# Half-height score passes made full-height, correction passes put in runs, and three order strings changed in a two-layer encoder

## The chip, the cores and the metric

The kernel runs on one core of a Trainium2 chip. Times are device microseconds (us) of that core, and lower is better. The core has a matrix engine (TensorE, PE in the rows; its weight loads stand apart as PEld), VectorE (DVE), ScalarE (ACT), GpSimd (POOL) and SyncE (SP, which issues the DMAs here).

## What is computed

A sequence of 256 tokens of width 1024 goes through two layers in fp32. Layer 0 mixes with a Hyena group (long convolutions by DFT) and eight heads of latent attention; layer 1 mixes with differential attention. Each layer then has a four-head cross-attention into 256 memory tokens and a squared-ReLU MLP of width 4096. What the change touches in layer 1:

```python
def diff_block_attention(q, k, v, lam):        # 16 half heads of width 64, 8 heads
    s = jnp.einsum('bqhd,bkhd->bhqk', qblk, k).astype(jnp.float32) * scale
    p = jax.nn.softmax(s, axis=-1).reshape(B, H, 2, Q_BLOCK, S)
    a = (p[:, :, 0] - lam * p[:, :, 1]).astype(v.dtype)      # two softmax maps a head
    return jnp.einsum('bhqk,bkhe->bqhe', a, v)
```

## The kernel before

**Arithmetic.** Nearly every product runs in a rounded fp32 format (fp32r) with a correction. An operand is split into `hi` (ACT rounds it, L110 or, with a gain, L105) and `lo` (DVE takes the rest, L111 or L106), and a product is hi·hi + hi·lo + lo·hi. `mm3` (L115 to L117) does this as three passes into one PSUM bank. A *pass* is one matmul instruction: a 128x128 weight tile is held and 128, 256 or 512 columns stream past.

**Side by side.** Where the moving operand is the activation (MLP up-projection, cross-attention queries, memory keys of layer 0), its `hi` and `lo` halves lie beside each other in 512 columns. `side_by_side` (L223 to L231) then needs two passes for a weight tile: one of 512 columns with the weight's `hi` (L229) and one of 256 columns with the weight's `lo` (L225). `proj_w4` calls it for four PSUM banks `c`, four weight groups `i` and two tiles `k` a group, bank by bank; `mem_k2` for two banks, two groups and four tiles. So a 512-column pass and a 256-column pass take turns. `joined` then adds the two halves of each bank on ACT and DVE. `Gained` splits the next stage's activation: three of its quarters as soon as they exist, the last one (`flush`) behind the first weight group of the next projection.

**Differential heads.** `qkv` turns q and k by position, transposes them (L886) and splits them into tiles `qkT`, in which one half head fills partitions 0 to 63 and its partner 64 to 127. `od_a` makes the two score maps of a head: for each token half `t` and each half head `m` one `mm3` on 64 partitions and 256 columns, twelve passes a head and 96 in all, into one bank for each `m`. A softmax (`softmax_e`) runs on each bank, and DVE combines the two maps with the factor lambda.

**Order.** Steps of a stage are named by letters, and strings set the order in which they are written (`ORDER_EVEN`, `ORDER_CROSS`, `ORDER_ODD`): in a cross-attention `Q` is a query projection, `K` and `V` keys and values of the memory, `S` the scores of a head, `B` its transposes (L455) and value product, `W` a part of the output projection; in the differential layer `Q` is `qkv`, `A`, `B`, `C` are the three steps of a head. A scheduler then lays the instructions on the engines' queues, and it moves filling work (memory keys of a later stage, weight splits) between them. The engines take their queues in order.

Of the kernel before, what the change touches and what calls it, by code (L numbers as in the profile page):

```python
# [10 lines left out]
F32 = mybir.dt.float32  # L11
BF16 = mybir.dt.bfloat16
F32R = mybir.dt.float32r
AF = mybir.ActivationFunctionType
ALU = mybir.AluOpType
AX = mybir.AxisListType

P = 128
D = 1024
EPS = 1e-6  # L20
SUBLN_EPS = 1e-5
# [3 lines left out]
C1 = 6.28125  # L25
C2 = float(np.float32(TWO_PI - C1))
C3 = float(np.float32(TWO_PI - C1 - C2))
PI_LO = 3.1415925

ORDER_EVEN = "X J H0 L U K G R S0 D H1 F0 S1 T0 S2 S3 P0 O0 O1 O2 H2 S4 O3 H3 T1 F1 S5 S6 O4 O5 Y S7 H4 P1 H5 O6 O7 M W"  # L30
ORDER_CROSS = [
    "Q0 V0 K0 K1 S0 B0 K2 S1 Q1 K3 S2 W0 V2 B1 S3 B2 B3 W1",
    "K0 K1 Q0 V0 S0 S1 K2 B0 Q1 K3 S2 V1 B1 V2 B2 W0 V3 S3 B3 W1",
]
ORDER_ODD = "Q2 Q0 Q1 A0 A1 B0 A2 C0 B1 B2 Q4 C1 C2 Q3 A3 A4 Q5 A5 B3 B4 C3 A6 C4 B5 B6 C5 A7 W0 W1 C6 B7 C7"


@with_exitstack
def tile_encoder(ctx: ExitStack, tc: tile.TileContext, a: dict, out: bass.AP):
    nc = tc.nc  # L40
# [19 lines left out]
    def wk():  # L60
        return T(ps, [P, 512], F32, "b", bufs=3)
# [47 lines left out]
    def split(hi, lo, src):  # L109
        nc.scalar.copy(hi, src)  # L110
        nc.vector.tensor_tensor(lo, src, hi.bitcast(F32), op=ALU.subtract)  # L111

    def mm3(o, l, r, first, last):
        (lh, ll), (rh, rl) = l, r
        nc.tensor.matmul(o, lh, rh, start=first, stop=False)  # L115
        nc.tensor.matmul(o, lh, rl, start=False, stop=False)  # L116
        return nc.tensor.matmul(o, ll, rh, start=False, stop=last)  # L117
# [28 lines left out]
    h = hilo()[:2]  # L146
    lat_all = t16(F32)
    lat_raw = [lat_all[:, i * 832:(i + 1) * 832] for i in range(4)]
    for c in range(2):
        for t in range(2):  # L150
            cs = slice(c * 512, (c + 1) * 512)
# [68 lines left out]
            if mid is not None and q == at:  # L220
                mid()

    def side_by_side(b, w, both, kk):  # L223
        def low():
            nc.tensor.matmul(b[:, :256], w[1], both[:, kk, 0, :], start=False, stop=False)  # L225

        if kk == 7:
            low()
        nc.tensor.matmul(v3(b, 2), w[0], both[:, kk], start=kk == 0, stop=kk == 7)  # L229
        if kk < 7:  # L230
            low()  # L231

    def proj_w4(h, src, banks, gi, mid=None):
        both = h[2]
        for i in range(4):
            wh, wl = (v3(z, 2) for z in weight(src[i], gi=(gi, 2 * i)))
            for c in range(4):
                for k in range(2):
                    side_by_side(banks[c], [z[:, k, c * P:(c + 1) * P] for z in (wh, wl)], both, 2 * i + k)
            if mid is not None and i == 0:  # L240
                mid()

# [41 lines left out]
    memB = T(cst, [P, 8, 2, 256], F32R, "memB")  # L284
# [9 lines left out]
    def mem_k2(l, u):  # L294
        bs = [wk(), wk()]
        for i in range(2):
            wh, wl = (v3(z, 4) for z in weight(a["xa_wk"][l, u, i]))
            for c in range(2):
                for k in range(4):
                    side_by_side(bs[c], [z[:, k, c * P:(c + 1) * P] for z in (wh, wl)], memB, 4 * i + k)  # L300
        y = joined(*bs)
        k = [T(rp, [P, 2, 256], F32R, f"kTm{i}", bufs=2) for i in range(2)]
        split(k[0], k[1], y)
        return k
# [122 lines left out]
        return (ec, es_), (pc, ps_)  # L427


    def softmax_e(sc, scale=None):  # L430
        s3 = v3(sc, 2)
        nm = col(2)
        nc.vector.reduce_max(nm, s3, axis=AX.X, negate=True)
        if scale is not None:
            nc.vector.tensor_tensor(nm, nm, scale, op=ALU.mult)
        e3 = v3(t2(), 2)
        su = col(2)
        for m in range(2):
            nc.scalar.activation(e3[:, m, :], s3[:, m, :], AF.Exp, bias=nm[:, m:m + 1],
                                 scale=1.0 if scale is None else scale[:, m:m + 1], accum_out=su[:, m:m + 1])  # L440
        return e3, su
# [40 lines left out]
    R = T(ep, [P, 256], F32, "rrow")  # L482
# [101 lines left out]
    qT = []  # L584
# [111 lines left out]
    def mla_proj():  # L696
# [4 lines left out]
        J=lat_proj, L=latents, U=queries, K=keys_values, R=queries_T, D=tables, G=features_2, X=rope_gains)  # L701
    ys, banks = hs["y"], hs["b"]
    cat = hilo()[:2]
    for u in range(2):
        b = hb()
        b4 = b.rearrange("p (c t n) -> p c t n", c=2, t=2)
        for c in range(2):
            cs = slice((2 * u + c) * P, (2 * u + c + 1) * P)
# [3 lines left out]
        z = v3(h2(), 2)  # L712
# [119 lines left out]
    op = pool("op", os_, reuse_waits="tile")  # L832
# [20 lines left out]
    CD, SD = rope[:, :, 64:128], rope[:, :, 128:192]  # L853
    vo = [T(op, [P, 2, 512], F32, f"vo{j}") for j in range(2)]
    qkT = {}

    def qkv(i):
        j, part = divmod(i, 3)
        banks = [hb(), hb()]
        proj_xs(h, a["od_w_qkv"][2 * part + j], 512, banks, 1, cur_.flush)  # L860
        if part == 2:
            for t in range(2):
                nc.scalar.activation(vo[j][:, t, :], banks[t], AF.Identity, bias=zero, scale=rs[:, t:t + 1])
            return
        rt = rq if part == 0 else rs
        rows = []
        for t in range(2):
            src = banks[t].rearrange("p (h d) -> p h d", d=64)
            r, tmp = t2(), t2()
            r3, m3 = (z.rearrange("p (h d) -> p h d", d=64) for z in (r, tmp))  # L870

            def turned(dst, s_, tab):
                tab = tab.unsqueeze(1).to_broadcast([P, 8, tab.shape[-1]])
                nc.vector.scalar_tensor_tensor(dst, s_, rt[:, t:t + 1], tab, op0=ALU.mult, op1=ALU.mult)

            turned(m3[:, :, :32], src[:, :, 32:], SD[:, t, :32])
            turned(m3[:, :, 32:], src[:, :, :32], SD[:, t, 32:])
            turned(r3, src, CD[:, t, :])
            nc.vector.tensor_tensor(r, r, tmp, op=ALU.add)
            rows.append(r)  # L880
        for u in range(2):
            b = v3(wk(), 2)
            for c in range(2):
                for t in range(2):
                    cs = slice((2 * u + c) * P, (2 * u + c + 1) * P)
                    nc.tensor.transpose(b[:, c, t * P:(t + 1) * P], rows[t][:, cs], ident)  # L886
            dT = [T(op, [P, 2, 256], F32R, f"qkT{part}{i_}", bufs=3) for i_ in range(2)]
            split(*dT, b)
            qkT[part, 2 * j + u] = dT

    st, banks_o = {}, []
# [1 line left out]
    def od_a(hd):  # L893
        j, c = divmod(hd, 4)
        q, k = qkT[0, hd // 2], qkT[1, hd // 2]
        c %= 2
        av = t2()
        a3 = v3(av, 2)
        es_, su = [], []
        bs = [wk(), wk()]  # L900
        for t in range(2):
            for m in range(2):
                rows = slice(64 * m, 64 * m + 64)
                mm3(bs[m][:, t * 256:(t + 1) * 256], [z[rows, c, t * P:(t + 1) * P] for z in q], [z[rows, c, :] for z in k],
                    True, True)
        for b in bs:
            e3, s_ = softmax_e(b)
            es_.append(e3)
            su.append(s_)
        w = col(2)  # L910
        nc.vector.reciprocal(w, su[1])
        nc.vector.scalar_tensor_tensor(w, w, nlam, su[0], op0=ALU.mult, op1=ALU.mult)
        eps = T(op, [P, 2], F32, "eps", bufs=4)
        nc.vector.scalar_tensor_tensor(eps, su[0], SUBLN_EPS, su[0], op0=ALU.mult, op1=ALU.mult)
        for t in range(2):
            nc.vector.scalar_tensor_tensor(a3[:, t, :], es_[1][:, t, :], w[:, t:t + 1], es_[0][:, t, :],
                                           op0=ALU.mult, op1=ALU.add)
        st[hd] = a3, eps

# [180 lines left out]
```

## Time and profile before

| what | value |
|---|---|
| three runs | 851.22, 853.45 and 853.88 us, median 853.45 us |
| the profiled execution | 852.3 us, of it span of the trace 850.5 us |
| PE busy | 829.4 us, 98% of the span, 4514 passes |
| weight loads, DVE, ACT busy | 695.0, 586.6 and 508.2 us |
| POOL busy | 19.5 us |
| DMA | 138.89 MB, 163 GB/s mean |
| chain that ended last | 79% on PE, 11% issue, 4% ACT, 2% DVE, 2% DMA |

The end of a pass is modelled, so rows of PE overlap: a pass of 512 columns is shown with some 0.39 us although the next one starts 0.23 us later. What a pass costs is therefore read from start to start, not from its duration.

### The profile page before, as it was taken

The page shows a single profiled execution, that of the slowest core. Times are in us where ns is not written, and L with a number is a line of the kernel's source. Part 1 is how long each engine was busy: PE and PEld are TensorE (multiplying, and loading weights), DVE is VectorE, ACT ScalarE, POOL GpSimd, SP SyncE. Part 2 cuts the span into 40 slices and gives each one's busy share as a digit, 9 for nine tenths or more (in the row PEclk, how much of TensorE's full clock was granted, in tenths as well). Part 3 has the DMA queues.
Part 4 walks back from the last instruction along what each step waited for, and adds up shares of the span by engine and source line. Part 5 has one row for each costly group of instructions (what it writes and reads, how often), then busy time and mean ns, then how long its engine had stood idle before and what let it go on. Part 6 is the DMA issues. An engine that isn't in the chain of part 4 may idle for free.

```text
span 850.5 us, 12079 instructions
## 1 busy us (share of the span) xinstructions
PE 829.4 (98%) x4514; PEld 695.0 (82%) x4514; DVE 586.6 (69%) x940; ACT 508.2 (60%) x883; POOL 19.5 (2%) x51
## 2 busy tenths in 40 slices
PE   6999999999999999999999999999999999999996
PEld 5867587788888888888888788889998888888885
DVE  4978796876658666666668888677654776666663
ACT  5896464766447555555567667666543755555542
POOL 0010000000000000000000010100000000000000
PEclk9999999999999999999999999999999999999998
DMA  7660317765527666666647416245522566656641
GB/s 275 199 207 19 121 36 263 236 209 159 170 68 218 202 187 190 192 191 186 196 132 226 153 66 198 75 145 178 159 90 100 168 201 189 189 191 184 191 125 50
DMA packets 39519, 138.89 MB, mean 163 GB/s; under 512 B 4515, under 2 KB 5155, under 8 KB 39461
## 3 DMA queue, kind: packets, MB, share of 16 engines
q1 hardware_dynamic: 39460, 138.13, 51.6%
q8 instruction: 35, 0.57, 0.3%
q14 instruction: 24, 0.19, 0.1%
HBM read 137.06 MB, written 1.05 MB: 162 GB/s over the span
## 4 chain that ended last, share of the span: by engine, by line
PE 79%; issue 11%; ACT 4%; DVE 2%; DMA 2%; POOL 1%; SPq 0%; POOLq 0%; ACTq 0%; DVEq 0%
PE h L115 12%; PE h L116 12%; PE h L117 12%; PE b L229 11%; PE b L225 5%; PE h L229 4%; PE f L229 3%; PE b L115 2%; PE h L225 2%; PE b L116 2%; PE b L117 2%; PE f L115 2%; PE f L116 2%; PE f L117 2%; PE f L225 2%
## 5 line engine op out<-in xcount | busy, mean ns | idle before, releaser
L111 DVE TENSOR_TENSOR wlo<-wraw,whi 128x1024 fp32r<-128x1024 f32 (+1 forms) x127 | 153.9, 1218 | 100.9 <-ACT whi L110 100.3
L110 ACT CAST whi<-wraw 128x1024 fp32r<-128x1024 f32 (+1 forms) x127 | 132.5, 1048 | 124.0 <-PE f L229 42.7
L105 ACT ACTIVATE whi<-wraw,zero,cpack 128x512 fp32r<-128x512 f32 x208 | 160.0, 811 | 62.6 <-PE h L117 20.3
L106 DVE SCALAR_TENSOR_TENSOR wlo<-wraw,cpack,whi 128x512 fp32r<-128x512 f32 x208 | 150.3, 749 | 42.8 <-ACT whi L105 42.6
L229 PE MATMUL b<-t,whi 128*128 128x512 f32 x336 | 119.5, 398 | 0.0
L117 PE MATMUL h<-whi,ul 128*128 128x512 f32 x256 | 99.9, 390 | 0.0
L115 PE MATMUL h<-whi,uh 128*128 128x512 f32 x256 | 99.6, 389 | 0.0
L116 PE MATMUL h<-wlo,uh 128*128 128x512 f32 x256 | 99.6, 389 | 0.0
L225 PE MATMUL b<-t,wlo 128*128 128x256 f32 x336 | 87.3, 280 | 0.0
L115 PE MATMUL h<-whi,t 128*128 128x512 f32 x192 | 76.8, 401 | 0.0
L116 PE MATMUL h<-wlo,t 128*128 128x512 f32 x192 | 76.5, 399 | 0.0
L117 PE MATMUL h<-whi,t 128*128 128x512 f32 x192 | 76.0, 397 | 0.0
L229 PEld LDWEIGHTS b<-t,whi 128*128 128x128 f32 x336 | 61.1, 188 | 12.2
L229 PE MATMUL h<-t,whi 128*128 128x512 f32 x192 | 67.9, 400 | 1.4 <-DVE t L111 1.4
L225 PEld LDWEIGHTS b<-t,wlo 128*128 128x128 f32 x336 | 63.4, 189 | 3.7
L116 PEld LDWEIGHTS h<-wlo,uh 128*128 128x128 f32 x256 | 48.0, 188 | 10.1
L117 PEld LDWEIGHTS h<-whi,ul 128*128 128x128 f32 x256 | 48.1, 188 | 9.9
L115 PEld LDWEIGHTS h<-whi,uh 128*128 128x128 f32 x256 | 48.1, 188 | 9.3
L225 PE MATMUL h<-t,wlo 128*128 128x256 f32 x192 | 50.0, 281 | 0.0
L229 PE MATMUL f<-t,whi 128*128 128x512 f32 x112 | 42.7, 398 | 0.0
L117 PEld LDWEIGHTS h<-whi,t 128*128 128x128 f32 x192 | 36.1, 188 | 7.2 <-DVE t L111 0.2
L115 PEld LDWEIGHTS h<-whi,t 128*128 128x128 f32 x192 | 36.1, 188 | 7.0
(325 smaller groups left out, 1633.1 us busy)
## 6 DMA issues: line engine op xcount, KB each, us to landing
wraw<-in_mlp_up_dram SPq DMA_DIRECT2D x64, 512.0 KB, 4.2
wraw<-in_mlp_down_dram SPq DMA_DIRECT2D x64, 512.0 KB, 4.3
wraw<-in_od_w_qkv_dram SPq DMA_DIRECT2D x24, 512.0 KB, 4.3
wraw<-in_xa_wq_dram SPq DMA_DIRECT2D x16, 512.0 KB, 4.1
wraw<-in_xa_wo_dram SPq DMA_DIRECT2D x16, 512.0 KB, 4.2
wraw<-in_w_hy_dram SPq DMA_DIRECT2D x12, 512.0 KB, 4.0
wraw<-in_w_out_ev_dram SPq DMA_DIRECT2D x8, 512.0 KB, 4.4
wraw<-in_xa_wv_dram SPq DMA_DIRECT2D x8, 512.0 KB, 5.4
```

What stands on the lines that cost most here:

```text
L105: nc.scalar.activation(h_, r_, AF.Identity, bias=zero, scale=g)
L106: nc.vector.scalar_tensor_tensor(l_, r_, g, h_.bitcast(F32), op0=ALU.mult, op1=ALU.subtract)
L110: nc.scalar.copy(hi, src)
L111: nc.vector.tensor_tensor(lo, src, hi.bitcast(F32), op=ALU.subtract)
L115: nc.tensor.matmul(o, lh, rh, start=first, stop=False)
L116: nc.tensor.matmul(o, lh, rl, start=False, stop=False)
L117: return nc.tensor.matmul(o, ll, rh, start=False, stop=last)
L225: nc.tensor.matmul(b[:, :256], w[1], both[:, kk, 0, :], start=False, stop=False)
L229: nc.tensor.matmul(v3(b, 2), w[0], both[:, kk], start=kk == 0, stop=kk == 7)
```

## The change

1. `side_by_side` is rewritten. It now gets all banks of a weight group, and the passes of one width stand in a row: all 512-column passes (`high`), then all 256-column ones (`low`), and in every second group the other way round, so that equal widths meet at the border of two groups. The last group goes bank by bank.
2. The k of a differential head no longer shares 256 columns between two half heads. A tile `apart` of 512 columns, filled with zeros by POOL, takes half head 0 in partitions 0 to 63 of its first 256 columns and half head 1 in partitions 64 to 127 of its last 256. Its split is done for each half (two on ACT, two on DVE, instead of one each). One `mm3` of 512 columns on all 128 partitions then gives both score maps of a token half: six passes a head, 48 in all. Banks and softmaxes now go by token half.
3. In all three order strings steps change places.

```diff
-ORDER_EVEN = "X J H0 L U K G R S0 D H1 F0 S1 T0 S2 S3 P0 O0 O1 O2 H2 S4 O3 H3 T1 F1 S5 S6 O4 O5 Y S7 ..."
+ORDER_EVEN = "X J H0 L U K R S0 G D H1 F0 S1 T0 S2 P0 S3 O0 O1 O2 H2 S4 O3 H3 T1 F1 S6 S5 O4 O5 Y S7 ..."
-    "Q0 V0 K0 K1 S0 B0 K2 S1 Q1 K3 S2 W0 V2 B1 S3 B2 B3 W1",
+    "Q0 V0 K0 K2 S0 K1 B0 V2 S1 Q1 K3 S2 B1 W0 S3 B2 B3 W1",
-ORDER_ODD = "... Q5 A5 B3 B4 C3 A6 C4 B5 B6 C5 A7 W0 W1 C6 B7 C7"
+ORDER_ODD = "... Q5 B3 A5 B4 C3 A6 C4 B6 B5 C5 A7 W0 W1 C6 B7 C7"
...
+    def side_by_side(banks, w, both, k0):
+        wh, wl = w
+        nk = wh.shape[1]
+        last = k0 + nk == 8
+        def high(c, k):
+            nc.tensor.matmul(v3(banks[c], 2), wh[:, k, c * P:(c + 1) * P], both[:, k0 + k],
+                             start=k0 + k == 0, stop=last and k == nk - 1)
+        def low(c, k):
+            nc.tensor.matmul(banks[c][:, :256], wl[:, k, c * P:(c + 1) * P], both[:, k0 + k, 0, :],
+                             start=False, stop=False)
+        every = range(len(banks))
+        for cs in [(c,) for c in every] if last else [every]:
+            for one in (low, high) if k0 // nk % 2 else (high, low):
+                for c in cs:
+                    for k in range(nk):
+                        one(c, k)
...
+    apart = [[T(op, [P, 2, 512], F32R, f"apart{i}{j}", bufs=1) for j in range(2)] for i in range(3)]
+    for z in apart:
+        for y in z:
+            nc.gpsimd.memset(y.bitcast(F32), 0.0)
...
-            dT = [T(op, [P, 2, 256], F32R, f"qkT{part}{i_}", bufs=3) for i_ in range(2)]
-            split(*dT, b)
+            if part == 0:
+                dT = [T(op, [P, 2, 256], F32R, f"qT{i_}", bufs=3) for i_ in range(2)]
+                split(*dT, b)
+            else:
+                dT = apart[(2 * j + u) % 3]
+                for m in range(2):
+                    half = slice(64 * m, 64 * m + 64)
+                    split(*(z[half, :, m * 256:(m + 1) * 256] for z in dT), b[half])
...
-        for t in range(2):
-            for m in range(2):
-                rows = slice(64 * m, 64 * m + 64)
-                mm3(bs[m][:, t * 256:(t + 1) * 256], [z[rows, c, t * P:(t + 1) * P] for z in q], [z[rows, c, :] for z in k],
-                    True, True)
-        for b in bs:
-            e3, s_ = softmax_e(b)
-            es_.append(e3)
-            su.append(s_)
+        su = T(op, [P, 2, 2], F32, "su", bufs=4)
+        for t in range(2):
+            b = wk()
+            mm3(b, [z[:, c, t * P:(t + 1) * P] for z in q], [z[:, c, :] for z in k], True, True)
+            es_.append(softmax_e(b, None, su[:, t, :])[0])
```

**PE, first weight group of the first query projection of layer 0's cross-attention** (h_1503 to h_1506 are its four banks, whi and wlo the weight, t the activation). Before:

```order
L229 MATMUL h_1503<-t_297_1388,whi_1509 128x512
L225 MATMUL h_1503<-t_297_1388,wlo_1510 128x256
L229 MATMUL h_1503<-t_297_1388,whi_1509 128x512
L225 MATMUL h_1503<-t_297_1388,wlo_1510 128x256
L229 MATMUL h_1504<-t_297_1388,whi_1509 128x512
```

Changed:

```order
L229 MATMUL h_1503<-t_297_1388,whi_1509 128x512 x2
L229 MATMUL h_1504<-t_297_1388,whi_1509 128x512 x2
L229 MATMUL h_1505<-t_297_1388,whi_1509 128x512 x2
L229 MATMUL h_1506<-t_297_1388,whi_1509 128x512 x2
L233 MATMUL h_1503<-t_297_1388,wlo_1510 128x256 x2
L233 MATMUL h_1504<-t_297_1388,wlo_1510 128x256 x2
```

Alternating widths have become eight passes of 512 and eight of 256 columns.

**PE, the transposes of step B1 of layer 0's cross-attention and what follows them** (b_2264 and b_2224 take the transposes, b_2271 and b_2231 the value product that needs them; h_2246 to h_2249 are banks of the output projection). Before:

```order
L117 MATMUL b_2183<-whi_2240,memB_91 128x512
L455 MATMUL b_2264<-cpack_70,t_401_1937 128x128 x4
L115 MATMUL b_2271<-t_468_2262,vp_355_1702 128x256
L115 MATMUL b_2286<-kTm_435_2114,qT_2059 128x256
L116 MATMUL b_2286<-kTm_436_2115,qT_2059 128x256
```

Changed:

```order
L459 MATMUL b_2224<-cpack_70,t_417_2017 128x128 x4
L115 MATMUL h_2246<-whi_2252,t_317_1499 128x512
L116 MATMUL h_2246<-wlo_2253,t_317_1499 128x512
L117 MATMUL h_2246<-whi_2252,t_317_1499 128x512
L115 MATMUL h_2247<-whi_2252,t_317_1499 128x512
L116 MATMUL h_2247<-wlo_2253,t_317_1499 128x512
L117 MATMUL h_2247<-whi_2252,t_317_1499 128x512
L115 MATMUL h_2248<-whi_2252,t_317_1499 128x512
L116 MATMUL h_2248<-wlo_2253,t_317_1499 128x512
L117 MATMUL h_2248<-whi_2252,t_317_1499 128x512
L115 MATMUL h_2249<-whi_2252,t_317_1499 128x512
...
```

Seventeen passes of the output projection now stand between the transposes and the value product.

**POOL, start of the differential layer** (col_798 and col_799 are the row scales of the layer's norm, L173 and L175 make them). Before:

```order
L173 TENSOR_SCALAR col_798_4096<-col_775_3978 128x2
L175 TENSOR_TENSOR col_799_4098<-col_798_4096,mhalf_86 128x2
L943 TENSOR_TENSOR col_905_4538<-col_892_4496,eps_4450 128x2
```

Changed:

```order
L863 MEMSET apart_804_4105 128x1024
L863 MEMSET apart_805_4106 128x1024
L863 MEMSET apart_806_4107 128x1024
L863 MEMSET apart_807_4108 128x1024
L173 TENSOR_SCALAR col_798_4096<-col_775_3978 128x2
L863 MEMSET apart_808_4109 128x1024
L175 TENSOR_TENSOR col_799_4098<-col_798_4096,mhalf_86 128x2
L863 MEMSET apart_809_4110 128x1024
```

Five of the six zero fills stand ahead of the end of the norm's scale.

## Rows read from the trace of the kernel before

**Rows 1.** Page: engine, busy us (share of the span) xinstructions; granted clock in 40 slices.

```profile
PE 829.4 (98%) x4514; PEld 695.0 (82%) x4514; DVE 586.6 (69%) x940; ACT 508.2 (60%) x883; POOL 19.5 (2%) x51
...
PEclk9999999999999999999999999999999999999998
```

**Rows 2.** Waits of PE: engine line <- waited for: us in total, times, longest.

```profile
PE h L229 <- DVE t L111: 1.4, 2, 1.1
```

**Rows 3.** PE groups: line engine op names shapes xcount | busy us, mean ns.

```profile
L229 PE MATMUL b<-t,whi 128*128 128x512 f32 x336 | 119.5, 398 | 0.0
...
L229 PE MATMUL h<-t,whi 128*128 128x512 f32 x192 | 67.9, 400 | 1.4 <-DVE t L111 1.4
...
L229 PE MATMUL f<-t,whi 128*128 128x512 f32 x112 | 42.7, 398 | 0.0
...
L229 PE MATMUL b<-memB,whi 128*128 128x512 f32 x64 | 22.6, 398 | 0.1
```

**Rows 4.** PE timeline, query projection: start us, us, engine line op out<-in xcount.

```profile
199.28 0.28 PE L225 MATMUL h<-t,wlo 128*128 128x256 f32 x1
...
202.11 0.28 PE L225 MATMUL h<-t,wlo 128*128 128x256 f32 x1
...
202.81 0.40 PE L225 MATMUL h<-t,wlo 128*128 128x256 f32 x2
...
204.92 0.39 PE L225 MATMUL h<-t,wlo 128*128 128x256 f32 x2
```

**Rows 5.** PE timeline: 48 equal passes of 512 columns, B1 behind them, 48 of 256.

```profile
217.91 0.39 PE L115 MATMUL b<-whi,memB 128*128 128x512 f32 x1
...
228.79 0.60 PE L455 MATMUL b<-cpack,t 128*128 128x128 f32 x4
230.12 0.39 PE L115 MATMUL b<-t,vp 128*128 128x256 f32 x1 [0.73 <-ACT t L110]
...
565.90 0.28 PE L115 MATMUL f<-memB,fhi 128*128 128x256 f32 x1
...
571.66 0.40 PE L229 MATMUL h<-t,whi 128*128 128x512 f32 x1
```

**Rows 6.** PE group of the half-height score passes (L116 and L117 have as many).

```profile
L115 PE MATMUL b<-qkT,qkT 64*128 64x256 f32 x32 | 9.2, 327 | 0.0
```

**Rows 7.** PE timeline around score stretches of 1, 17 and 6 passes: two neighbours each.

```profile
474.33 0.40 PE L116 MATMUL h<-wlo,t 128*128 128x512 f32 x1
...
475.31 0.39 PE L115 MATMUL h<-whi,t 128*128 128x512 f32 x1
...
476.23 0.40 PE L116 MATMUL h<-wlo,t 128*128 128x512 f32 x1
...
478.64 0.39 PE L116 MATMUL h<-wlo,t 128*128 128x512 f32 x1
...
546.73 0.40 PE L115 MATMUL h<-whi,t 128*128 128x512 f32 x1
...
548.54 0.39 PE L117 MATMUL h<-whi,t 128*128 128x512 f32 x1
```

**Rows 8.** POOL groups: the zero fills that there are.

```profile
L536 POOL MEMSET kp<- 128x64 f32 x2 | 0.2, 151 | 0.0
...
L560 POOL MEMSET edge<- 128x2 f32 x2 | 0.2, 102 | 0.0
```

**Rows 9.** PE, POOL and DVE timelines at the start of the differential layer.

```profile
434.13 0.40 PE L117 MATMUL h<-whi,ul 128*128 128x512 f32 x1
...
437.68 0.36 POOL L173 TENSOR_SCALAR col<-col 128x2 f32<-128x2 f32 x1 [284.66 <-ACT junk L199]
...
438.86 0.17 DVE L852 TENSOR_SCALAR col<-col 128x2 f32<-128x2 f32 x1 [0.61 <-POOL col L175]
...
439.73 0.68 DVE L111 TENSOR_TENSOR t<-b,t 128x512 fp32r<-128x512 f32 x1
...
440.97 0.39 PE L115 MATMUL h<-whi,t 128*128 128x512 f32 x1
```

More of the change, by code (lines that the diff above doesn't have):

```diff
@@ L28 @@
 PI_LO = 3.1415925
-ORDER_EVEN = "X J H0 L U K G R S0 D H1 F0 S1 T0 S2 S3 P0 O0 O1 O2 H2 S4 O3 H3 T1 F1 S5 S6 O4 O5 Y S7 H4 P1 H5 O6 O7 M W"
+ORDER_EVEN = "X J H0 L U K R S0 G D H1 F0 S1 T0 S2 P0 S3 O0 O1 O2 H2 S4 O3 H3 T1 F1 S6 S5 O4 O5 Y S7 H4 P1 H5 O6 O7 M W"
 ORDER_CROSS = [
-    "Q0 V0 K0 K1 S0 B0 K2 S1 Q1 K3 S2 W0 V2 B1 S3 B2 B3 W1",
+    "Q0 V0 K0 K2 S0 K1 B0 V2 S1 Q1 K3 S2 B1 W0 S3 B2 B3 W1",
     "K0 K1 Q0 V0 S0 S1 K2 B0 Q1 K3 S2 V1 B1 V2 B2 W0 V3 S3 B3 W1",
 ]
-ORDER_ODD = "Q2 Q0 Q1 A0 A1 B0 A2 C0 B1 B2 Q4 C1 C2 Q3 A3 A4 Q5 A5 B3 B4 C3 A6 C4 B5 B6 C5 A7 W0 W1 C6 B7 C7"
+ORDER_ODD = "Q2 Q0 Q1 A0 A1 B0 A2 C0 B1 B2 Q4 C1 C2 Q3 A3 A4 Q5 B3 A5 B4 C3 A6 C4 B6 B5 C5 A7 W0 W1 C6 B7 C7"
 @with_exitstack
@@ L221, in proj_xs @@
                 mid()
[L223 to L231, printed above, removed]
+    def side_by_side(banks, w, both, k0):
[14 more added lines that the diff above has]
+                        one(c, k)
     def proj_w4(h, src, banks, gi, mid=None):
-        both = h[2]
         for i in range(4):
[L236 to L239, printed above, removed]
+            w = [v3(z, 2) for z in weight(src[i], gi=(gi, 2 * i))]
+            side_by_side(banks, w, h[2], 2 * i)
             if mid is not None and i == 0:
@@ L296, in mem_k2 @@
         for i in range(2):
[L297 to L300, printed above, removed]
+            side_by_side(bs, [v3(z, 4) for z in weight(a["xa_wk"][l, u, i])], memB, 4 * i)
         y = joined(*bs)
@@ L427, in spectrum, with softmax_e @@
         return (ec, es_), (pc, ps_)
-    def softmax_e(sc, scale=None):
+    def softmax_e(sc, scale=None, su=None):
         s3 = v3(sc, 2)
@@ L436, in softmax_e @@
         e3 = v3(t2(), 2)
-        su = col(2)
+        su = col(2) if su is None else su
         for m in range(2):
@@ L898, in od_a @@
         a3 = v3(av, 2)
-        es_, su = [], []
-        bs = [wk(), wk()]
+        es_ = []
+        su = T(op, [P, 2, 2], F32, "su", bufs=4)
         for t in range(2):
-            for m in range(2):
-                rows = slice(64 * m, 64 * m + 64)
-                mm3(bs[m][:, t * 256:(t + 1) * 256], [z[rows, c, t * P:(t + 1) * P] for z in q], [z[rows, c, :] for z in k],
-                    True, True)
-        for b in bs:
-            e3, s_ = softmax_e(b)
-            es_.append(e3)
-            su.append(s_)
+            b = wk()
+            mm3(b, [z[:, c, t * P:(t + 1) * P] for z in q], [z[:, c, :] for z in k], True, True)
+            es_.append(softmax_e(b, None, su[:, t, :])[0])
         w = col(2)
-        nc.vector.reciprocal(w, su[1])
-        nc.vector.scalar_tensor_tensor(w, w, nlam, su[0], op0=ALU.mult, op1=ALU.mult)
+        nc.vector.reciprocal(w, su[:, :, 1])
+        nc.vector.scalar_tensor_tensor(w, w, nlam, su[:, :, 0], op0=ALU.mult, op1=ALU.mult)
         eps = T(op, [P, 2], F32, "eps", bufs=4)
-        nc.vector.scalar_tensor_tensor(eps, su[0], SUBLN_EPS, su[0], op0=ALU.mult, op1=ALU.mult)
+        nc.vector.scalar_tensor_tensor(eps, su[:, :, 0], SUBLN_EPS, su[:, :, 0], op0=ALU.mult, op1=ALU.mult)
         for t in range(2):
-            nc.vector.scalar_tensor_tensor(a3[:, t, :], es_[1][:, t, :], w[:, t:t + 1], es_[0][:, t, :],
+            nc.vector.scalar_tensor_tensor(a3[:, t, :], es_[t][:, 1, :], w[:, t:t + 1], es_[t][:, 0, :],
                                            op0=ALU.mult, op1=ALU.add)
```

## The prediction

> **What bounds the kernel now.** I read the page's line of engines first: PE is busy for 829.4 of the 850.5 us of the span, over 4514 passes, and the granted clock stands at 9 tenths or more in 39 of 40 slices, so at the upper of its two levels, 2.4 GHz [rows 1]. A change must therefore either take time out of PE's own stream or cut one of its few waits. The view of waits comes next: the only wait behind which a query projection stands, L229 on DVE's rest of the split L111, is worth 1.4 us in two places, the longest 1.1 [rows 2]. So the stream itself is what there is to gain, and the cost of a pass has to be read from start to start, since the modelled ends overlap.
>
> The timeline gives three prices. In a row of 48 equal passes of 512 columns, PE goes from 217.91 to 228.79, 0.227 us a pass; 48 equal passes of 256 columns go from 565.90 to 571.66, 0.120 us a pass [rows 5]. One of each is thus 0.347 us. Where the widths take turns, eight pairs go from 199.28 to 202.11, 0.354 us a pair; where two of a width stand together, six pairs go from 202.81 to 204.92, 0.352 [rows 4]. A turn costs little, but it is paid very often.
>
> **Runs of equal width.** The groups of L229 count 336 + 192 + 112 + 64 = 704 pairs [rows 3]. In a `proj_w4` of the new kernel 24 of 32 pairs stand in runs of eight to sixteen, and the last eight in twos; in `mem_k2` half stand in runs of eight, half of four. At the pace of the long runs all pairs would save 704 x 0.007 = 4.9 us; at the pace of the twos 704 x 0.002 = 1.4 us; nothing, if the pace depended on something else than the order. About three quarters are in long runs, some 78 were in twos already, and the runs are not as long as 48, so I take 3.4 us, nearer the upper end, because the runs of eight and more resemble [rows 5] more than the twos of [rows 4].
>
> The Trainium skill ("TensorE: Matmul & The Clock Gate", section "Back-to-back issue gap") gives a warm gap of N/2.4 + 2.5 ns, with no term for the width of the pass ahead; by it a pair would be about 325 ns in either order (an estimate from that page), and the runs would bring nothing. The trace differs from its size, 354 against 347 ns, and its figure for sustained passes of 512 columns, 131 ns, is not met either, the row has 227. That result of the rule is the first rival below.
>
> **Full-height scores.** The three lines of `mm3` have 32 passes each of 64 partitions and 256 columns [rows 6], 96 in all; in the timeline they stand in fifteen stretches (seven of 6 passes, two of 4, three of 1, one each of 17, 18 and 8). The modelled 327 ns say nothing of their cost, the neighbours do. I take the time from the start of a full pass ahead to the start of the second or third full pass behind, less 0.227 for each full pass that started in it [rows 7]. One alone: 475.31 - 474.33 = 0.98, less two passes, 0.53 us. Seventeen: 478.64 - 476.23 = 2.41, less three full passes in that stretch, 1.73, 0.10 each. Six: 548.54 - 546.73 = 1.81, less three, 1.13, 0.19 each. So a stretch costs about 0.10 a pass and some 0.5 for going in and out, of the single pass (0.53 - 0.10 = 0.43) as of the six (1.13 - 0.60 = 0.53). For the list that gives 7 x 1.13 + 1.73 + 1.8 + 3 x 0.53 + 2.7 (two of four at 0.85, the eight, partly abreast, at 1.0): 15.7 us. They become 48 passes of 512 columns on all partitions, at 0.227 to 0.229 us 10.9 to 11.0 us, with no going in and out. Saved: 4.7 us. As bounds, 96 x 0.10 = 9.6 us would make it a loss of 1.3, and 96 x 0.19 = 18.2 a gain of 7.3; the sum by stretches lies between.
>
> The trace shows the half-height passes two abreast only where the two half heads of a head are mixed, as in the seventeen, 0.10 us each against 0.120 for a full-height pass of 256 columns; in the sixes there is no gain of that sort. The Trainium skill ("TensorEngine Tiling (Array Packing)", section "Theoretical Speedup") speaks against this change: a contraction of at most 64 makes two row tiles, up to twice as fast, which by 0.120 us a pair would be 48 x 0.120 = 5.8 us for the 96, and the new passes a loss of 5.1. The same page, "Key Properties", says that a change of mode drains the array, and the half us a stretch agrees with that.
>
> The new splits of k are two halves of 64 partitions, but each half still has 512 columns. So each of the four splits adds one cast on ACT and one rest on DVE. They run one behind the other, so what a late split could cost PE is one more DVE rest, 0.68 us [rows 9], 2.7 us for four. I count nothing: thirteen passes of the value projection, 13 x 0.227 = 3.0 us, stand between the first k's transposes and the first scores, against some 2 us for two casts and two rests (0.68 each, the casts taken as no longer) of which half overlaps. If that cover fails the price is the 2.7 us. The number of softmaxes is the same, and the first now starts after three passes instead of nine, so I count neither gain nor loss.
>
> **Order strings.** In layer 0's cross-attention the value product of B1 stands 230.12 - 228.79 = 1.33 us behind its four transposes, with 0.73 us idle on ACT's split [rows 5]; the four transposes need about 0.4. Seventeen passes of the output projection now stand in between, 17 x 0.227 = 3.9 us of cover: -0.9 us. In layer 1's cross-attention the 48 passes of 256 columns (L115 to L117) stood ahead of the L229 pass at 571.66 [rows 5], between the first weight group of Q0 and the rest, and covered the late quarter of the split. In the new order eleven of them stand ahead of Q0 and the other 37 behind it, so the split has only one weight group to hide behind. The same wait elsewhere is 0 to 1.1 us [rows 2]; I take the middle, +0.6. The first query projection of layer 0's cross-attention now asks for its fourth bank a little earlier, but the 1.1 us wait of [rows 2] stands right behind it and takes that up: the end of the wait is set by the split. The moves in layer 0's first stage exchange passes with each other; I count 0, with 1 us either way.
>
> **Zero fills.** POOL is nearly idle, 19.5 us [rows 1], but it takes its queue in order, and the norm's scale is in it. Four fills stand ahead of L173, the fifth ahead of L175, and L852 on DVE waits for L175; behind that on DVE stands the late split L111, which PE wants at 440.97 [rows 9]. A fill has 1024 columns; those of 2 and 64 columns took 102 and 151 ns [rows 8], 0.8 ns a column, so m = 0.9 us (an estimate). The first can start when the last down pass, at 434.13, has been read, about 434.55 [rows 9]. Then L173 starts at 434.55 + 4m = 438.2 instead of 437.68, L852 1.18 + m later (1.18 is 438.86 - 437.68), and the split ends some 0.9 us behind that: 441.2, 0.2 us late. I count +0.2. From there each further us of m costs 5 us.
>
> **Sum.** -3.4 - 4.7 - 0.9 + 0.6 + 0.2 = -8.2 us. On the profiled execution, 852.3 us (1.8 of it outside the span), this gives 844.1; on the median of the runs, 853.45, which stands 1.1 above it, 845.3. I say 844.7.
>
> **Rivals.** All times are against the 844.1.
> 1. The pace of a pair doesn't follow the order, and the runs bring nothing: 844.1 + 3.4 = 847.5. For it: the twos gained only 2 of 7 ns. Against: both long rows of [rows 5] are faster than any mixed stretch. It is also where the Trainium skill's gap formula leads ("TensorE: Matmul & The Clock Gate", "Back-to-back issue gap").
> 2. The split halves come late: 844.1 + 2.7 = 846.8. For it: ACT and DVE are busy 60 to 69%; against: the thirteen passes ahead of the first scores.
> 3. More comes back: all runs at the full pace (-1.4), no wait at Q0 (-0.6), layer 0's new order gaining 1: about 841.1.
> 4. The half-height passes are cheaper than I read, because what I charge to going in and out is in the neighbours anyway: 5.1 lost instead of 4.7 gained, 844.1 + 9.8 = 853.9, no change. For it: the stretches of 17. Against: the single pass between full ones, 0.53 us. The Trainium skill's page on tiling is on its side.
> 5. Slower: POOL's fills hold the norm's scale back. With a fill of m the split ends at 434.55 + 5m + 2.1, so PE waits 5m - 4.3 us. Without the 0.2, the rest gains 8.4: gone at m = 2.5, and from m = 3.1 the kernel is slower by over 0.3%, 854.9 us and more on the scale of the profiled execution. For it: 1024 columns lie far from 64, and the price is drawn out sixteenfold. Against: two rows fix the slope, and it would have to be four times as steep.
>
> **How the numbers follow.** A measurement of this kernel can tell about 0.3%, 2.6 us, from no change: on the scale of the profiled execution the bounds are 849.7 and 854.9. My forecast has 0.68, rival 1 0.10, rival 2 0.07, rival 3 0.07, rival 4 0.03, rival 5 0.05 (0.03 beyond 854.9, 0.02 within the bounds). Faster: 0.68 + 0.10 + 0.07 + 0.07 = 0.92; same 0.03 + 0.02 = 0.05; slower 0.03. The range goes from rival 3, 841, up to rivals 1 and 2 together, 844.1 + 6.1 = 850.2, say 850.
>
> **What would show it.** In the timeline of the new kernel, passes of L229 and L233 inside a run should start 0.227 and 0.120 us apart; 0.236 and 0.118 would mean rival 1. The score passes should be 48 of 128 x 512 at 0.23 us, without steps of 0.33 around them. No idle time of 0.7 us ahead of the value product behind L459. A fill on POOL near 0.9 us, and PE not idle for more than half a us near 441. An idle time under 1.1 us behind the first weight group of Q0 in the last cross-attention. I am wrong if PE's passes keep their old steps, or if waits of PE on splits or on POOL's scale add up to more than 4 us.

## The result: 846.8 us, and where the gain lies

The changed kernel takes 846.82 us in the median against 853.45 for the kernel before; the ratio is 0.9919, interval 0.9898 to 0.9939. Beside the last experiments it ran once more: 845.30 against 853.88 on that chip, ratio 0.9901 (0.9888 to 0.9915). So it is faster by 6.6 to 8.6 us, where the prediction said 844.7 and -8.2. One of the five runs of the first measurement took 2896.41 us, at a granted clock of 1.0; the ratio leaves it out, and no trace shows why it was long. The total was well met. The terms of the sum were not: the heads brought 1.8 of their 4.7 us in their own stretch, and an order string that had been counted at nothing brought 2 to 4.

The page after, beside [rows 1]: the engines and the granted clock.

```profile
PE 822.5 (98%) x4466; PEld 694.0 (82%) x4466; DVE 592.6 (70%) x944; ACT 512.9 (61%) x887; POOL 24.6 (3%) x57
...
PEclk9999999999999999999999999999999999999999
```

PE has 48 passes less, 6.9 us less busy time, and the span is 7.0 us shorter; the page's line of the clock reads as before. To see where, the program is cut at passes that both kernels have: the first transposes (L181) of layer 0's cross-attention, of the first MLP, of the differential layer and of the second MLP, and the last down pass. The timeline of PE before (start us, us, engine, line, operation), and the same five marks after:

```profile
139.37 0.33 PE L181 MATMUL h<-cpack,t 128*128 128x128 f32 x1 [0.47 <-DVE t L278]
246.42 0.33 PE L181 MATMUL b<-cpack,t 128*128 128x128 f32 x1
425.91 0.27 PE L181 MATMUL b<-cpack,t 128*128 128x128 f32 x1
656.03 0.33 PE L181 MATMUL b<-cpack,t 128*128 128x128 f32 x1
842.31 0.39 PE L117 MATMUL h<-whi,ul 128*128 128x512 f32 x1
```

```profile
137.33 0.33 PE L181 MATMUL h<-cpack,t 128*128 128x128 f32 x1 [1.09 <-DVE t L285]
242.66 0.33 PE L181 MATMUL b<-cpack,t 128*128 128x128 f32 x1
421.05 0.27 PE L181 MATMUL b<-cpack,t 128*128 128x128 f32 x1
650.11 0.33 PE L181 MATMUL b<-cpack,t 128*128 128x128 f32 x1
835.29 0.39 PE L117 MATMUL h<-whi,ul 128*128 128x512 f32 x1
```

The differences of neighbouring marks, for these two and, read in the same way, for the experiments (us):

| kernel | front | cross-attention 0 | MLP 0 | differential and cross-attention 1 | MLP 1 |
|---|---|---|---|---|---|
| before | 139.37 | 107.05 | 179.49 | 230.12 | 186.28 |
| changed | 137.33 | 105.33 | 178.39 | 229.06 | 185.18 |
| changed, run again | 137.36 | 105.13 | 178.38 | 228.24 | 185.18 |
| runs alone | 139.16 | 106.65 | 178.38 | 230.05 | 185.17 |
| heads alone | 140.09 | 106.81 | 179.47 | 228.35 | 186.27 |
| three strings alone | 136.41 | 106.56 | 179.47 | 230.02 | 186.26 |
| layer 0's first string alone | 138.40 | 105.68 | 179.48 | 230.13 | 186.27 |
| changed, without the heads | 137.97 | 105.70 | 178.35 | 229.74 | 185.18 |

The MLPs repeat to 0.04 us. The front does not: over all fourteen profiles it ends at 138.7 to 140.1 with the old string of layer 0 (four profiles) and at 136.4 to 139.0 with the new one (ten), so a single profile tells no difference under some 2.6 us there, and the medians are used. A part of this is the clock. In eight of the fourteen profiles the granted clock was at the lower of its two levels, 1.2 GHz, for a few us between 30 and 40 us, in the other six it was not. The window from 30 to 35 us shows it in the first profile of the changed kernel (length; PE, PEld, DVE, ACT and POOL busy; granted clock, 0.70 here and 1.00 before; DMA share and GB/s):

```profile
30.00:35.00 5.00, 3.94 (x13) 3.61 (x14) 3.90 (x9) 4.00 (x8) 0.00 (x0) 0.70 0.62 197
```

The stretch of the differential layer differs by 0.8 us between two profiles of one kernel.

### The profile page after: what moved, and what is told of

It reads as the page before. It is cut to its first block, busy times and chain, and to the rows that moved or that the text cites. A ratio compares the mean times of both kernels' runs of the same rounds, so it can differ in the third digit from the quotient of the medians.

```text
span 843.5 us, 11999 instructions
## 1 busy us (share of the span) xinstructions
PE 822.5 (98%) x4466; PEld 694.0 (82%) x4466; DVE 592.6 (70%) x944; ACT 512.9 (61%) x887; POOL 24.6 (3%) x57
## 4 chain that ended last, share of the span: by engine, by line
PE 75%; issue 12%; ACT 5%; DVE 3%; DMA 2%; POOL 1%; SPq 0%; POOLq 0%; ACTq 0%; DVEq 0%
PE h L115 11%; PE h L117 11%; PE h L116 11%; PE b L229 11%; PE b L233 6%; PE h L229 4%; PE f L229 3%; PE b L115 2%; PE b L117 2%; PE b L116 2%; PE h L233 2%; PE f L115 2%; PE f L117 2%; PE f L116 2%; PE f L233 2%
## 5 line engine op out<-in xcount | busy, mean ns | idle before, releaser
L111 DVE TENSOR_TENSOR wlo<-wraw,whi 128x1024 fp32r<-128x1024 f32 (+1 forms) x127 | 153.7, 1217 | 94.8 <-ACT whi L110 91.8
L117 PE MATMUL h<-whi,ul 128*128 128x512 f32 x256 | 99.9, 390 | 0.0
L116 PE MATMUL h<-wlo,uh 128*128 128x512 f32 x256 | 99.6, 389 | 0.0
L115 PE MATMUL h<-whi,uh 128*128 128x512 f32 x256 | 99.6, 389 | 0.0
L229 PE MATMUL b<-t,whi 128*128 128x512 f32 x336 | 90.7, 392 | 0.0
L115 PE MATMUL h<-whi,t 128*128 128x512 f32 x192 | 76.6, 399 | 0.7 <-ACT t L958 0.7
L116 PE MATMUL h<-wlo,t 128*128 128x512 f32 x192 | 76.3, 397 | 0.0
L117 PE MATMUL h<-whi,t 128*128 128x512 f32 x192 | 75.8, 396 | 0.0
L229 PEld LDWEIGHTS b<-t,whi 128*128 128x128 f32 x336 | 59.3, 189 | 9.0
L116 PEld LDWEIGHTS h<-wlo,uh 128*128 128x128 f32 x256 | 48.1, 188 | 10.1
L115 PEld LDWEIGHTS h<-whi,uh 128*128 128x128 f32 x256 | 48.1, 188 | 9.9
L117 PEld LDWEIGHTS h<-whi,ul 128*128 128x128 f32 x256 | 48.1, 188 | 9.9
L233 PEld LDWEIGHTS b<-t,wlo 128*128 128x128 f32 x336 | 49.8, 190 | 4.7
L233 PE MATMUL b<-t,wlo 128*128 128x256 f32 x336 | 53.5, 282 | 0.0
L229 PE MATMUL h<-t,whi 128*128 128x512 f32 x192 | 51.0, 395 | 0.7 <-DVE t L111 0.7
L115 PEld LDWEIGHTS h<-whi,t 128*128 128x128 f32 x192 | 36.1, 188 | 7.7 <-ACT t L958 1.3
L117 PEld LDWEIGHTS h<-whi,t 128*128 128x128 f32 x192 | 36.1, 188 | 6.9
L116 PEld LDWEIGHTS h<-wlo,t 128*128 128x128 f32 x192 | 36.2, 188 | 6.5
L229 PEld LDWEIGHTS h<-t,whi 128*128 128x128 f32 x192 | 33.5, 188 | 6.8 <-DVE t L111 1.8
```

The costliest lines, as they stand in the source:

```text
L229: nc.tensor.matmul(v3(banks[c], 2), wh[:, k, c * P:(c + 1) * P], both[:, k0 + k], start=k0 + k == 0, stop=last and k == nk - 1)
L233: nc.tensor.matmul(banks[c][:, :256], wl[:, k, c * P:(c + 1) * P], both[:, k0 + k, 0, :], start=False, stop=False)
```

## Experiments

**The runs of equal width alone.** `side_by_side` and its two callers are the new ones; all else is as before.

```diff
-    def side_by_side(b, w, both, kk):
+    def side_by_side(banks, w, both, k0):
...
+            for one in (low, high) if k0 // nk % 2 else (high, low):
+                for c in cs:
+                    for k in range(nk):
+                        one(c, k)
```

> The kernel before with the runs of equal width alone (side_by_side and its two callers); score passes and order strings as before. Theory P (the forecast): 704 pairs, each 4 to 5 ns cheaper, 2.8 to 3.4 us; against the 850.5 us span of before that is 847.1 to 847.7, and each MLP (transposes ahead of it to its last down pass) is 1.1 us shorter. Rival (the pace of a pair does not follow the order, and the MLPs were shortened by something else): 850 to 851, MLPs unchanged.

Measured: 850.72 us against 852.99, ratio 0.9976 (0.9964 to 0.9988), so 1.0 to 3.1 us; the span is 2.9 us shorter. Each MLP is 1.11 us shorter, which is 4.3 ns for each of its 256 pairs. One block of an up-projection shows it: 32 pairs from the first L229 pass to the first down pass. Before, then changed:

```profile
267.02 0.39 PE L229 MATMUL b<-t,whi 128*128 128x512 f32 x1
...
278.28 0.39 PE L115 MATMUL h<-whi,uh 128*128 128x512 f32 x1
```

```profile
263.14 1.52 PE L229 MATMUL b<-t,whi 128*128 128x512 f32 x6
...
264.96 0.88 PE L233 MATMUL b<-t,wlo 128*128 128x256 f32 x6
...
274.27 0.39 PE L115 MATMUL h<-whi,uh 128*128 128x512 f32 x1
```

11.26 us have become 11.13, 352 ns a pair 348. Inside the run eight passes of 512 columns go from 263.14 to 264.96, 0.228 each, where those of the alternating pairs of [rows 4] took 0.236 on average. The pace does follow the order; the rival by which it does not is out. The new order also changes banks more often than the old one; the 48 passes of [rows 5], of which `mm3` puts three in a row into a bank, take 0.227 as well, which speaks for the widths and not the banks, but no run separates the two.

**The heads alone.** Zero-filled k, full-height passes and softmaxes by token half, with the old strings.

```diff
+                dT = apart[(2 * j + u) % 3]
+                for m in range(2):
+                    half = slice(64 * m, 64 * m + 64)
+                    split(*(z[half, :, m * 256:(m + 1) * 256] for z in dT), b[half])
...
+            mm3(b, [z[:, c, t * P:(t + 1) * P] for z in q], [z[:, c, :] for z in k], True, True)
```

> The kernel before with the full-height score passes alone (zero-filled k, one pass for both maps, softmax by token half). Theory P (the passes give 4.7 us and only the moved order string of the differential layer took it away again): span 850.5 - 4 to 5 = 845.5 to 846.5. Theory Q (the passes give some 3 us, and the longer chain of a head, two half splits and a softmax for each token half, leaves PE waiting some 1.5 us in any order): about 849. Rival 5 of the forecast (fills hold back the norm's scale) would show PE idle near 437 to 441 us.

Measured: 851.26 us against 852.99, ratio 0.9972 (0.9962 to 0.9981), 1.6 to 3.2 us; in its own stretch 1.77 us (228.35 for 230.12). The numbers of theory Q come out, theory P falls. The view of PE's waits for that stretch of the kernel before, and of the heads alone (engine, line, waited for: us in total, times, longest):

```profile
PE b L948 <- DVE t L946: 0.5, 1, 0.5
PE h L229 <- DVE t L111: 0.3, 1, 0.3
```

```profile
PE b L953 <- DVE t L951: 1.1, 3, 0.5
PE h L115 <- ACT t L954: 0.4, 1, 0.4
PE b L939 <- ACT t L941: 0.4, 2, 0.2
```

0.8 us of waits have become 1.9. The passes themselves thus gave 1.8 + 1.1 = 2.9 us, and PE spends 1.1 of it waiting for the last steps of a head: the scaling on DVE (L951), the rounding on ACT (L954), the squares (L941). The scaling itself waits for POOL's power (L949): DVE is idle for it for 6.2 us in four places, where the kernel before has 2.8 in three (L944).

**The three strings alone.**

```diff
-ORDER_EVEN = "X J H0 L U K G R S0 D ..."
+ORDER_EVEN = "X J H0 L U K R S0 G D ..."
...
-ORDER_ODD = "... Q5 A5 B3 B4 C3 A6 C4 B5 B6 ..."
+ORDER_ODD = "... Q5 B3 A5 B4 C3 A6 C4 B6 B5 ..."
```

> The kernel before with the three order strings alone. If the steps of the forecast are right: value product of B1 -0.9, the first stage of layer 0 about -1.4 (its part in the new kernel's trace, less 0.6 that is a shorter first load of x), the differential layer and its cross-attention 0 to +0.6: 848.5 to 849. If the new waits of the differential layer (0.46, 0.66, 0.27 and 0.24 us) belong to the order string: +1.5 there, and 850 in all.

Measured: 848.73 us against 852.99, ratio 0.9947 (0.9935 to 0.9959), 3.5 to 5.5 us. This is the largest of the three parts, and the forecast had it at -0.3. The differential layer is unchanged (230.02), so by itself the string there makes no wait that shows.

**The changed kernel without the heads** (half-height passes, runs and strings as changed).

```diff
-            mm3(b, [z[:, c, t * P:(t + 1) * P] for z in q], [z[:, c, :] for z in k], True, True)
+            for m in range(2):
+                rows = slice(64 * m, 64 * m + 64)
+                mm3(bs[m][:, t * 256:(t + 1) * 256], [z[rows, c, t * P:(t + 1) * P] for z in q], [z[rows, c, :] for z in k],
+                    True, True)
```

> The changed kernel with half-height score passes, as before (runs and order strings kept). It prices the heads in the new order. If the heads are worth the 4.7 us of the forecast: span 843.5 + 4.7 = 848. If they are worth only what the two traces show for the differential layer and its cross-attention together, about 1 us: 844.5. If the order string costs 1.5 us only together with the new heads: below 843.5.

Measured: 846.91 us against 852.99, ratio 0.9923 (0.991 to 0.9935); the stretch is 229.74 us, 0.7 to 1.5 longer than in the two profiles of the changed kernel. The heads are worth about 1 us there, not 4.7.

**The differential layer's string put back, and each of its two swaps.** First both swaps undone:

```diff
-ORDER_ODD = "... Q5 B3 A5 B4 C3 A6 C4 B6 B5 C5 ..."
+ORDER_ODD = "... Q5 A5 B3 B4 C3 A6 C4 B5 B6 C5 ..."
```

> The changed kernel with the differential layer's order string of before. Between the transposes at the end of the first MLP and those at the start of the second, the changed kernel takes 229.06 us with 2.5 us of waits of PE, the heads alone in the old order 228.35 us with 1.9. If the moved string makes the new waits: 228.3 in that stretch, 0.7 us less in all, and the waits on L443 and on the last step of a head are gone. If the waits come with the heads in any order: 229.0, no difference.

Measured: 845.34 us against 853.26, ratio 0.9905 (0.989 to 0.9919), the stretch 227.96. That looked like the 0.7 to 1.1 us of the string. Then one swap at a time, beside the changed kernel itself:

> The changed kernel once more, beside the others of this call. Its stretch between the two MLPs was 229.06 us; 229.0 to 229.1 again would show that this part repeats, and how far the front (first MLP's start) moves shows what of a profile's front is chance. Median 846 to 847.

> The changed kernel with only the first of the two swaps in the differential layer's string (B3 ahead of A5; B5 and B6 as before). With neither swap the stretch between the MLPs is 227.96 us, with both 229.06. If this swap carries the loss (the wait of 0.46 us of B's transposes on the exponentials would then be here): 229.0 and a median as the changed kernel's; if not: 228.0, about 1 us less.

> The changed kernel with only the second swap (B6 ahead of B5). If it carries the loss (the wait of 0.66 us on the last step of a head would then be here): 229.0 in the stretch between the MLPs and a median as the changed kernel's; if not: 228.0. If each carries half: 228.5 in both.

Measured, all against 853.88: the changed kernel 845.30 (0.9888 to 0.9915), stretch 228.24; the first swap 845.45 (0.9889 to 0.9918), 228.38; the second 843.83 (0.9866 to 0.9898), 227.74. Neither swap carries a loss, and the changed kernel itself now takes 0.8 us less than its first 229.06. The waits of the same stretch, first profile and second:

```profile
PE b L957 <- DVE t L955: 1.0, 3, 0.5
PE h L115 <- ACT t L958: 0.7, 1, 0.7
PE b L936 <- ACT t L443: 0.5, 1, 0.5
PE h L229 <- DVE t L111: 0.2, 1, 0.2
```

```profile
PE b L957 <- DVE t L955: 0.9, 3, 0.5
PE h L115 <- ACT t L958: 0.7, 1, 0.7
PE h L229 <- DVE t L111: 0.3, 1, 0.3
```

The wait of 0.5 us on the exponentials (L443) is not there the second time, in the same program. So the 227.96 can't be told from the spread of runs, and this string is neutral within what these runs can tell. The second swap alone has the best median, but its interval overlaps that of the changed kernel: it isn't shown to be better.

**Layer 0's first string put back, and alone.**

```diff
-ORDER_EVEN = "X J H0 L U K R S0 G D H1 F0 S1 T0 S2 P0 S3 ..."
+ORDER_EVEN = "X J H0 L U K G R S0 D H1 F0 S1 T0 S2 S3 P0 ..."
```

> The changed kernel with layer 0's first order string of before. Theory E (that string brings some 2 us, which the forecast counted as 0): median 2 to 2.5 us above the changed kernel's 846.8, and all of it ahead of the first cross-attention. Theory N (the front of the kernel varies by 2 us from run to run with the first load of x and the granted clock, and the string brings nothing): within 0.7 us of 846.8.

Measured: 849.32 us against 853.26, ratio 0.9959 (0.9943 to 0.9976), 2.5 us above the first median of the changed kernel and 4.0 above the second. Alone in the kernel before:

> The kernel before with layer 0's first order string alone. The changed kernel lost 2.5 us when that string was put back, and the three strings alone gained 4.3. Theory E (this string carries most of it, by itself): 2.5 to 3 us below the kernel before. Theory I (it does so only together with the runs or with the cross-attention's string): under 1 us.

Measured: 849.99 us against 853.88, ratio 0.9962 (0.9949 to 0.9975), so 2.1 to 4.4 us by itself. Theory E holds in both directions. Where it goes, two stretches ahead of the cross-attention show: from the L115 pass that waits for ACT (L553) to the L467 pass, and from there to the transposes L181. Before, then with this string alone:

```profile
34.13 0.44 PE L115 MATMUL b<-whi,latT 128*128 128x384 f32 x1 [0.94 <-ACT t L553]
...
81.70 0.41 PE L467 MATMUL h<-cpack,hy 128*128 128x128 f32 x2 [0.47 <-DVE hy L580]
...
124.98 0.50 PE L116 MATMUL f<-wlo,catm 128*128 128x512 f32 x1 [0.75 <-DVE wlo L111]
```

```profile
34.15 0.44 PE L115 MATMUL b<-whi,latT 128*128 128x384 f32 x1 [0.94 <-ACT t L553]
...
50.40 3.67 PE L385 MATMUL h<-t,aT 128*128 128x512 f32 x8 [0.67 <-DMA t<-in_hy_w_dram]
...
81.26 0.41 PE L467 MATMUL h<-cpack,hy 128*128 128x128 f32 x2 [0.48 <-DVE hy L580]
...
138.40 0.33 PE L181 MATMUL h<-cpack,t 128*128 128x128 f32 x1 [1.03 <-DVE t L278]
```

The second stretch, less the wait at its end, is 139.37 - 81.70 - 0.47 = 57.20 us before and 138.40 - 81.26 - 1.03 = 56.11 with the string. All four profiles with the old string have 57.18 to 57.21 there and all ten with the new one 56.10 to 56.13: 1.1 us, of which 0.75 is the wait on a weight's split (L116), which stands in all of the four and in none of the ten. The first stretch is 47.57 us before and 47.11 with the string, of which 0.67 is a new wait on a load (L385). Among the six profiles without the lower clock it is 47.5 to 47.6 with the old string, and 46.4 to 46.5 with the new one less that wait, which is 0.2 to 0.8 us long: another 1.1 us, partly handed back. Where the clock was low, the new string has 47.4 to 47.7 in its place. So some 1.4 to 2 us of this string are located; the rest of the 2.1 to 4.4 is not. The wait at the transposes L181 itself is 0.5 to 1.0 us with the old string and 0.3 to 1.3 with the new one. The 1.1 us wait of the query projection [rows 2] is not settled by it: it is gone in the profile of this string alone, but that of the three strings still has it:

```profile
152.72 0.50 PE L229 MATMUL h<-t,whi 128*128 128x512 f32 x1 [1.12 <-DVE t L111]
```

**One half of k alone.** Only the first half head of each k is split, so ACT and DVE have as many splits as in the kernel before; the scores of every second half head are left out.

```diff
-                for m in range(2):
+                for m in range(1):
                     half = slice(64 * m, 64 * m + 64)
```

> The changed kernel that splits only the first half head of each k; the other half stays at the zeros of the fill, so the scores of every second half head are zero: that part of the computation is left out. ACT and DVE have as many splits as before. Theory S (the added half splits make the new waits of the differential layer): PE's waits there fall from 2.5 us to about 1, the stretch from 229.06 to 227.6. Theory C (PE waits because its own score passes are shorter and the chain of max, exponentials and combination is as long as before): waits within 0.5 us of 2.5.

Measured once: 844.81 us, the stretch 228.44, with these waits:

```profile
PE b L957 <- DVE t L955: 0.7, 2, 0.5
PE f L115 <- DVE kTm L111: 0.6, 1, 0.6
PE b L181 <- DVE t L285: 0.4, 1, 0.4
```

That is 1.7 us, against 2.4 and 1.9 in the two profiles of the changed kernel, and the stretch lies between theirs. Theory S asked for about 1, theory C for 2.0 to 3.0; neither is met. Only 0.7 of it stands at the steps of a head, against 2.2 and 1.6; the other 1.0 is on a sum and a split behind the heads (L285, L111), where the changed kernel has 0.2 to 0.3. So the half splits may well hold up the heads, with the time lost again further on. In the next experiment, though, PE waits as long at the heads without any half split. This run decides for neither theory, and no run took a step out of the chain of a head: what makes these waits stays open.

**Half-height passes in pairs.** The two half heads' passes take turns, without fills and half splits.

```diff
-                mm3(bs[m][:, t * 256:(t + 1) * 256], [z[rows, c, t * P:(t + 1) * P] for z in q], [z[rows, c, :] for z in k],
-                    True, True)
+            abreast([(bs[m][:, t * 256:(t + 1) * 256], [z[rows, c, t * P:(t + 1) * P] for z in q],
+                      [z[rows, c, :] for z in k]) for m, rows in enumerate(halves)])
```

> The changed kernel with half-height score passes, but those of the two half heads taking turns, each pair on the two halves of the array (no fills, no half splits). From the mixed stretches of the kernel before, a pair takes 0.12 us and an unbroken stretch of twelve some 1.1 us, against 6 x 0.23 = 1.4 us for a head at full height. Theory of the two row tiles: 1 to 2 us shorter than the full-height kernel, 845 to 846. Rival (the scheduler splits the stretches and each entry and exit costs 0.4 to 0.5 us): as with plain half-height passes, 846.9.

Measured: 847.72 us against 853.26, ratio 0.9932 (0.9919 to 0.9946), no better than full height (0.9901 to 0.9919) and the stretch 230.63 us, with 1.7 us of waits at the steps of a head. The rival's time comes out. The timeline of PE shows a stretch of both half heads:

```profile
473.17 0.39 PE L116 MATMUL h<-wlo,t 128*128 128x512 f32 x1
473.49 1.58 PE L122 MATMUL b<-qkT,qkT 64*128 64x256 f32 x17
...
475.33 0.40 PE L115 MATMUL h<-whi,t 128*128 128x512 f32 x1
```

Seventeen passes cost 475.33 - 473.17 less two full passes, 1.71 us; the next stretch, six passes, costs 478.05 - 476.49 less two, 1.11. In [rows 7] it is 1.73 and 1.13. These rows don't tell the two half heads apart. That the scheduler still puts passes of one half head in a row, so that few stand beside a partner, is inferred from the times: both stretches cost what they did in the kernel before. The factor of up to two that the Trainium skill ("TensorEngine Tiling (Array Packing)", section "Theoretical Speedup") gives for a contraction of at most 64 is therefore not reached here. The drain at a change of mode, which its "Key Properties" name, agrees with the trace: the full pass ahead of each of these two stretches has its neighbour 0.32 us behind it, where equal passes have 0.227.

## Why the prediction held in the sum and not in its terms

**What bounds the kernel.** Right: PE is still 98% busy, and all that was gained came out of its stream or its few waits.

**Runs, -3.4.** The mechanism was right and the size nearly: 4.3 ns a pair in the MLPs, where the long rows of [rows 5] against [rows 4] gave 7 as the most and the sum took 4.9; 704 pairs at 4.3 are 3.0 us. The spans say -2.9, the median -2.3.

**Heads, -4.7.** This term failed: -1.8 in the stretch when made alone, -0.7 to -1.5 in the changed kernel. Two steps of it are to blame. The first is the price of the stretches, 15.7 us. I charged every entry and exit to the half height, as beside full passes in [rows 7]. But 12 of the 30 borders lie at transposes or value products of 128 columns, seven of them on the way in, and there a full-height pass makes a step too. The kernel before, four such passes and two half-height ones behind them:

```profile
486.40 0.60 PE L934 MATMUL b<-vo,t 128*128 128x128 f32 x4
486.94 0.39 PE L115 MATMUL b<-qkT,qkT 64*128 64x256 f32 x2
487.16 0.28 PE L116 MATMUL b<-qkT,qkT 64*128 64x256 f32 x1
```

and the changed kernel, four such passes and one full-height one:

```profile
482.64 0.69 PE L943 MATMUL b<-vo,t 128*128 128x128 f32 x4
483.08 0.48 PE L115 MATMUL b<-apart,qT 128*128 128x512 f32 x1
483.40 0.39 PE L116 MATMUL b<-apart,qT 128*128 128x512 f32 x1
```

Both take 0.76 us from the first row to the last, so nothing was saved at that border; the first full-height pass takes 483.40 - 483.08 = 0.32 us. Inside a row the new passes were priced well: eight of them take 475.26 - 473.41 = 1.85 us, 0.231 each for 0.228, without steps of 0.33 around them:

```profile
473.41 0.39 PE L116 MATMUL b<-apart,qT 128*128 128x512 f32 x1
...
475.26 0.40 PE L116 MATMUL h<-wlo,t 128*128 128x512 f32 x1
```

With the heads alone, the 48 new passes take 11.75 us from start to start, waits left out, 0.8 more than the 10.9 to 11.0 of the forecast; seven of them take 0.31 or 0.32, six of these right behind 128-column passes. The half-height passes themselves had taken 12.4, so the 15.7 charged 3.3 us to their neighbours; the other passes of the stretch became only 2.2 us shorter. That is 0.8 + 1.1 = 1.9 of the missing 2.9 us. The step that is the same in either form is shown at the way in; why the neighbours gave 1.1 less is not shown pass by pass. (The price of a stretch is split wrongly, too: in the six of [rows 7] neighbouring passes start 0.12 us apart and not 0.10, which leaves 0.41 for going in and out and not 0.53. The sum goes by whole stretches and is not touched by it.) Rival 4, by which the heads lose 5.1 us, is out.

The second step is "I count neither gain nor loss" for the chain of a head: PE's waits there grow by 1.1 us, which is the rest. An argument for it is that PE comes sooner to each step behind the softmax while the chain on DVE, ACT and POOL is no shorter; the half splits are the other candidate, and the run with one half of k doesn't exclude them.

**The rival on late half splits** had the right sort of loss, but not where it was looked for: the waits stand at L953, L954 and L939, none on a split of k. Whether the added splits cause them by keeping ACT and DVE busy is open.

**Strings.** B1 is right. The product's wait of 0.73 us in [rows 5] is gone, with full passes now behind the transposes:

```profile
224.29 0.39 PE L116 MATMUL h<-wlo,t 128*128 128x512 f32 x1
224.75 0.38 PE L115 MATMUL b<-t,vp 128*128 128x256 f32 x1
```

The +0.6 for the last cross-attention did not come: the wait there is 0.24 us, as long as the one that was in its place before (the second of the two in [rows 2], 0.3).

```profile
571.01 0.50 PE L229 MATMUL h<-t,whi 128*128 128x512 f32 x1 [0.24 <-DVE t L111]
```

The term for layer 0's first string, "I count 0, with 1 us either way", failed by 2 to 4 us, as the two experiments show. The step behind it was that the moves "exchange passes with each other". The passes of the two stretches are the same ones, as far as the traces hold them all, but they take 2.2 us less in the new order, and 0.75 of that is a wait of a pass on a weight's split that I had not looked at and that the new order ended.

**Zero fills, +0.2.** The price of a fill was right, and the 0.2 us did not show. POOL, DVE and PE after, to be read beside [rows 9]:

```profile
429.74 3.64 POOL L863 MEMSET apart<- 128x1024 f32 x4 [279.45 <-PE h L117]
...
435.36 0.90 DVE L856 TENSOR_SCALAR col<-col 128x2 f32<-128x2 f32 x1 [1.01 <-POOL col L175]
435.44 0.83 DVE L111 TENSOR_TENSOR t<-b,t 128x512 fp32r<-128x512 f32 x1
...
436.11 0.39 PE L115 MATMUL h<-whi,t 128*128 128x512 f32 x1
```

Four fills take 3.64 us, 0.91 each; 0.9 had been drawn out of two rows of 2 and 64 columns [rows 8]. DVE waits 1.01 us for POOL instead of 0.61, and PE takes its pass at 436.11 without a wait. The slower rival, whose point lay at 3.1 us a fill, was far off.

So the forecast was met because +2.9 us in the heads and -2 to -4 us in the first string mostly cancelled, and that was luck. The range, 841 to 850, would have held with either miss alone.

## What to carry to other kernels

Price a mode or a border by taking the same border in the form that will stand there afterwards; the step beside a 128-column pass is there in either case. When PE's own work ahead of a dependent step is shortened, subtract the cover that this work gave: ask for each such step when its other input is ready, and whether that comes sooner too. And judge an order change between two marks that hold the same passes in both kernels, with the waits on loads and at the end taken off: such a stretch repeated to 0.03 us over ten profiles here, while the mark at its end moved by 2.6.

## What the runs showed that was not expected

The same program differs by 0.8 us in one stretch between two profiles, 0.5 of it one wait that is there or is not; a difference of that size between two kernels needs a repeat. The granted clock fell to its lower level for a few us early in some executions and not in others; with the new string of layer 0 that cost the first of the two stretches above 1.0 to 1.3 us. The DVE instruction of 2 columns (L856), 0.17 us in [rows 9], is shown with 0.90 us while the sixth fill runs on POOL; the next one started 0.08 us behind it all the same.
